# Two SwiGLU feed-forwards: parts two and three through Strassen's seven products

## The chip, the cores and the metric

The kernel runs on one core of a Trainium2 chip. The metric is the time of one execution on the device in microseconds (us), 1309.17 as the median of three runs. Beside the runs there is a profile of one execution. In it PE is the matrix engine, PEld its loading of stationary operands, DVE, ACT and POOL are the vector, scalar and GpSimd engines, and SP issues most DMAs.

## The reference

Two decoder layers work on 512 tokens of width 1024 in float32. Layer 0 mixes by a convolution module, layer 1 by differential attention. Each is followed by a feed-forward of width 2816 and a gated embedding:

```
def swiglu(x, w_gate, w_up, w_down):
    return (jax.nn.silu(x @ w_gate) * (x @ w_up)) @ w_down

    for i in range(DEPTH):
        h = h + (conformer_conv or diff_attention of rms_norm(h))
        u = rms_norm(h, ffn_norm_g[i])
        h = h + swiglu(u, ffn_w_gate[i], ffn_w_up[i], ffn_w_down[i])
        gate = jax.nn.sigmoid(rms_norm(h, ple_norm_g[i]) @ ple_w_gate[i])
        h = h + gate * (p[i] @ ple_w_proj[i])
```

The feed-forward (`ffn`) is the only part that changes, in both layers.

## The kernel before

All activations lie transposed: a tile is 128 features by 512 tokens, and `h` is eight such tiles. Each float32 operand of a large product is split in a high part (rounded to the type fp32r) and a low part (the rest), and a product is three matmuls: low weight with high activation, high with low, high with high (`mm3`, lines L155 to L157). Weights come as tiles of 128 x 1024 numbers (512 KB). `weight()` loads one through SP (L145) into one of two `wraw` buffers, ACT casts the high part into one of four `whi` buffers (L148), and DVE subtracts to get the low part into one of four `wlo` buffers (L150).

The feed-forward goes through its 2816 hidden features in three parts of 8, 8 and 6 hidden tiles. For each hidden tile a gate tile and an up tile of weights are loaded. Each is multiplied with the eight normalised inputs `norm.u` (in the `A` buffers, split in two): 8 x 3 matmuls over 512 tokens. DVE takes the sums out of PSUM and scales them by the row norm `rb` (L582, L584), ACT applies Silu, DVE multiplies (L585), and the hidden tile is split into a `B` buffer (L587, L588). After each part `linear` multiplies the hidden tiles with eight tiles of the down projection and adds to `h` (L592). In the last part each finished `h` tile also starts the next norm (`chunk`, L169, L170, squares, and POOL's sums, L189).

PSUM has eight banks: four `mm`, two `sc` and two `tp`, each 128 x 512. The order of the instructions on each engine is set by a planner at build time. Each engine then works through its own list strictly in that order and waits on semaphores; DMAs of SP and POOL are issued in the order of those engines' lists. Buffers are named by a tag (`C3`, `wk`, ...) with a number of copies; who takes a buffer waits until its last reader is done.

Of the kernel before, what the change touches and what calls it, by code (L numbers as in the profile page):

```python
# [12 lines left out]
F32 = mybir.dt.float32  # L13
F32R = mybir.dt.float32r
AF = mybir.ActivationFunctionType
ALU = mybir.AluOpType
# [4 lines left out]
P = 128  # L21
S = 512
D = 1024
NC = D // P
# [52 lines left out]
PACK = True  # L77
E1 = True
GLO = 1
QKV = (("q", 0, (0, 0, 0, 0)), ("v", 0, (0, 1, 1, 0)), ("q", 1, (1, 1, 2, 2)), ("q", 2, (0, 1, 2, 0)), ("v", 1, (1, 2, 2, 2)), ("q", 3, (0, 2, 0, 1)))  # L80


@with_exitstack
def trunk(ctx, tc, xT, pT, wts, diag, dww, vec, rel, onehot, lamv, out):
    nc = tc.nc
    V, A, G, T = nc.vector, nc.scalar, nc.gpsimd, nc.tensor
# [19 lines left out]
    big = lambda dt=F32, shape=(P, S): sb(list(shape), "big", 5, dt)  # L106
    f = lambda ap: ap.bitcast(F32)
# [6 lines left out]
    def col(name, i=0):  # L114
        a, _ = VEC[name]
        return vt[:, a + i : a + i + 1]
# [7 lines left out]
    t = wk()[:, 0:P]  # L124
# [4 lines left out]
    t = tp()  # L129
# [4 lines left out]
    wnext = [0]  # L134
    loaded = [None]

    def weight(n=1024, pieces=1, between=(), eng=V, after=None):
        i = wnext[0]
        wnext[0] += 1
        raw = sb([P, 1024], "wraw", 2)  # L140
        hi = sb([P, 1024], "whi", 4, F32R)
        lo = sb([P, 1024], "wlo", 4, F32R)
        for k in range(pieces):
            cut = slice(k * n // pieces, (k + 1) * n // pieces)
            loaded[0] = nc.sync.dma_start(raw[:, cut], wts[i, :, cut])  # L145
            if k < len(between):
                between[k]()
            A.copy(hi[:, cut], raw[:, cut])  # L148
            with tc.issue_after(after.ins) if after else nullcontext():
                eng.tensor_tensor(lo[:, cut], raw[:, cut], f(hi[:, cut]), ALU.subtract)  # L150
        return hi, lo

    def mm3(acc, a, b, first, last):
        (ah, al), (bh, bl) = a, b
        T.matmul(acc, al, bh, start=first, stop=False)  # L155
        T.matmul(acc, ah, bl, start=False, stop=False)  # L156
        return T.matmul(acc, ah, bh, start=False, stop=last)  # L157

    def wpart(w, k):
        return tuple(t[:, k * P : (k + 1) * P] for t in w)  # L160
# [5 lines left out]
    h = [sb([P, S], f"h{c}", 1) for c in range(NC)]  # L166
# [66 lines left out]
    norm = Norm("conv_g")  # L233
# [36 lines left out]
    y = []  # L270
# [160 lines left out]
    for c in range(NC):  # L431
        wa, wg = pairs[c]
        if c == 0:
            pg = half(wg)
            norm.diagonal()
            pa = half(wa)
            rb = norm.rows()
# [3 lines left out]
        if c > 0:  # L441
            pg = half(wg)
# [5 lines left out]
        tg, ta = big(), big()  # L448
# [114 lines left out]
    linear(NC, z, add_conv, 3, first=(None, last_add[0], scaled[1]))  # L563


    def ffn(norm, after):
        rb = None
        for at, (f0, n) in enumerate(PARTS):
            hid = []
            for i in range(n):  # L570
                wg, wu = weight(), weight()
                pg, pu = mm(), mm()
                for k in range(NC):
                    mm3(pg, wpart(wg, k), norm.u[k], k == 0, k == NC - 1)
                if rb is None:
                    norm.diagonal()
                for k in range(NC):
                    mm3(pu, wpart(wu, k), norm.u[k], k == 0, k == NC - 1)
                if rb is None:
                    rb = norm.rows()  # L580
                tg, tu = big(), big()
                V.tensor_tensor(tg, pg, rb, ALU.mult)  # L582
                A.activation(tg, tg, AF.Silu)
                V.tensor_tensor(tu, pu, rb, ALU.mult)  # L584
                V.tensor_tensor(tu, tu, tg, ALU.mult)  # L585
                hl = sb([P, 2, S], f"B{i}", 1, F32R)
                A.copy(hl[:, 0], tu)  # L587
                V.tensor_tensor(hl[:, 1], tu, f(hl[:, 0]), ALU.subtract)  # L588
                hid.append((hl[:, 0], hl[:, 1]))

            def add(m, acc):
                V.tensor_tensor(h[m], acc, h[m], ALU.add)  # L592
                if at == len(PARTS) - 1:
                    after.chunk(m)

            linear(n, hid, add, 2)

# [26 lines left out]
                gate(*part)  # L624

    n2 = Norm("ple_g0")
    ffn(norm, n2)
    norm = Norm("attn_g")
    ple(n2, pp, lambda m, cut: norm.chunk(m))

# [9 lines left out]
    for k in range(2):  # L640
        t = tp()
# [263 lines left out]
    norm = Norm("ffn_g1")  # L905
# [4 lines left out]

    linear(NC, ot, add_attn, 2, heads_until, step)
    n2 = Norm("ple_g1")
    ffn(norm, n2)

    def store(m, cut):
        nc.sync.dma_start(out[m][:, cut], h[m][:, cut])
# [30 lines left out]
def _layout(a):  # L947
# [25 lines left out]
    qkv = a["attn_w_qkv"][0]  # L973
    for what, at, _ in QKV:
        if what == "v":
# [70 lines left out]
```

## Time and profile before

| what | value |
|---|---|
| runs (median, lowest, highest) | 1309.17, 1309.03, 1310.07 us |
| the profiled execution, first to last instruction | 1308.0 us |
| what lies around that span, against the median | 1.2 us |
| PE busy | 1278.6 us (98%) in 5904 matmuls |
| DVE, ACT, POOL busy | 741.2 (57%), 522.1 (40%), 248.2 (19%) us |
| mean granted PE clock | 0.985 |
| DMA | 131.97 MB, 101 GB/s on average |

The feed-forward of layer 0 lies from about 230 to 584 us of the span (parts: hidden tiles to 316, 442 and 551, a down projection behind each), that of layer 1 from about 905 to 1258 us. A row of instruction groups names the line, engine and operation, what it writes and reads, its shape and count; then busy time, mean length of one in ns, and the idle time of the engine before it with what ended that. A busy PE is one with a matmul in its pipe; its pace is read from the starts of matmuls that follow each other.

### The profile page before, as it was taken

How to read it: one execution, taken by the hardware profiler on the slowest of the kernel's cores; microseconds unless marked ns; L12 is line 12 of the kernel's file. 1: busy time of each engine (PE TensorE's matmuls, PEld its weight loads, DVE VectorE, ACT ScalarE, POOL GpSimd, SP SyncE). 2: the span in 40 equal slices, each digit the busy share in tenths (PEclk: the TensorE clock that was granted, in tenths of full speed). 3: DMA queues.
4: the chain of work that ended last, by engine and by line, in shares of the span. 5: the costliest groups of instructions: out<-in, count | busy, mean ns of one | idle time of the engine just before them, and what ended most of it. 6: DMA issues, size and time to landing. Idle time of an engine off the chain costs nothing. (4 is left out here: it accounts for less than half of the span.)

```text
span 1308.0 us, 15405 instructions
## 1 busy us (share of the span) xinstructions
PE 1278.6 (98%) x5904; PEld 1055.7 (81%) x5904; DVE 741.2 (57%) x1142; ACT 522.1 (40%) x827; POOL 248.2 (19%) x207
## 2 busy tenths in 40 slices
PE   8999999999999999999999998999999999999998
PEld 5888678888888888888888886878888888888887
DVE  6898646444344434456678888845543344334445
ACT  5642445332122212254566667734332233223332
POOL 4754323000000000032335535122000000000030
PEclk8999889999999999999999998999999999999999
DMA  6654313322323232232222211213323223222231
GB/s 219 229 166 156 106 33 129 96 98 87 106 96 97 88 104 94 80 122 83 80 91 92 89 58 59 87 48 114 97 97 97 97 97 97 97 97 89 83 119 65
DMA packets 46838, 131.97 MB, mean 101 GB/s; under 512 B 5379, under 2 KB 9987, under 8 KB 46764
## 3 DMA queue, kind: packets, MB, share of 16 engines
q1 hardware_dynamic: 44640, 127.55, 29.6%
q10 hardware_dynamic: 2124, 3.43, 0.8%
q8 instruction: 46, 0.75, 0.2%
q14 instruction: 28, 0.23, 0.1%
HBM read 126.75 MB, written 4.21 MB: 100 GB/s over the span
## 5 line engine op out<-in xcount | busy, mean ns | idle before, releaser
L148 ACT CAST whi<-wraw 128x1024 fp32r<-128x1024 f32 (+2 forms) x214 | 218.6, 1026 | 566.3 <-PE mm L157 349.5
L155 PE MATMUL mm<-A,wlo 128*128 128x512 f32 (+1 forms) x1096 | 423.9, 391 | 4.8 <-ACT A L169 2.7
L156 PE MATMUL mm<-A,whi 128*128 128x512 f32 (+1 forms) x1096 | 428.0, 392 | 0.4
L157 PE MATMUL mm<-A,whi 128*128 128x512 f32 (+1 forms) x1096 | 425.3, 389 | 0.0
L150 DVE TENSOR_TENSOR wlo<-wraw,whi 128x1024 fp32r<-128x1024 f32 (+2 forms) x210 | 260.5, 1244 | 70.9 <-ACT whi L148 70.6
L155 PEld LDWEIGHTS mm<-A,wlo 128*128 128x128 f32 x1096 | 206.2, 188 | 49.6 <-DVE wlo L150 3.7
L156 PEld LDWEIGHTS mm<-A,whi 128*128 128x128 f32 x1096 | 206.6, 188 | 46.4 <-DVE A L170 3.0
L157 PEld LDWEIGHTS mm<-A,whi 128*128 128x128 f32 x1096 | 206.6, 188 | 43.1 <-issue 1.0
L189 POOL TENSOR_TENSOR acc<-acc,wk 128x512 f32<-128x512 f32 x42 | 67.4, 1604 | 787.7 <-issue 660.2
L156 PE MATMUL mm<-B,whi 128*128 128x512 f32 x352 | 137.5, 391 | 0.0
L157 PE MATMUL mm<-B,whi 128*128 128x512 f32 x352 | 137.5, 391 | 0.0
L155 PE MATMUL mm<-B,wlo 128*128 128x512 f32 x352 | 137.2, 392 | 0.0
L592 DVE TENSOR_TENSOR h<-mm,h 128x512 f32<-128x512 f32 x48 | 33.0, 691 | 122.7 <-PE mm L157 122.7
L584 DVE TENSOR_TENSOR big<-mm,rb 128x512 f32<-128x512 f32 x44 | 30.4, 691 | 126.2 <-PE mm L157 126.2
L582 DVE TENSOR_TENSOR big<-mm,rb 128x512 f32<-128x512 f32 x44 | 30.4, 691 | 99.4 <-PE mm L157 93.0
L157 PEld LDWEIGHTS mm<-B,whi 128*128 128x128 f32 x352 | 66.1, 188 | 14.6
L155 PEld LDWEIGHTS mm<-B,wlo 128*128 128x128 f32 x352 | 66.1, 188 | 14.2
L156 PEld LDWEIGHTS mm<-B,whi 128*128 128x128 f32 x352 | 66.0, 188 | 14.2
L157 PE MATMUL mm<-whi,A 128*128 128x512 f32 x192 | 75.6, 395 | 0.0
L156 PE MATMUL mm<-wlo,A 128*128 128x512 f32 x192 | 75.0, 396 | 0.0
L155 PE MATMUL mm<-whi,A 128*128 128x512 f32 x192 | 74.8, 397 | 0.0
L214 POOL TENSOR_TENSOR r<-v,mhalf 128x8 f32<-128x8 f32 (+1 forms) x31 | 47.4, 1529 | 122.8 <-DVE v L212 100.4
(198 smaller groups left out, 1402.0 us busy)
## 6 DMA issues: line engine op xcount, KB each, us to landing
wraw<-in_wts SPq DMA_DIRECT2D x194, 512.0 KB, 3.5
wraw<-in_wts SPq DMA_DIRECT2D x16, 384.0 KB, 2.9
D<-in_diag SPq DMA_DIRECT2D x22, 256.0 KB, 4.9
C<-in_diag SPq DMA_DIRECT2D x16, 256.0 KB, 4.7
h<-in_xT SPq DMA_DIRECT2D x8, 256.0 KB, 5.6
bias<-scr ACTq DMA_DIRECT2D x8, 256.0 KB, 3.3
out_t<-h SPq DMA_DIRECT2D x7, 256.0 KB, 2.0
wraw<-in_wts SPq DMA_DIRECT2D x4, 256.0 KB, 5.2
```

Of the source, the lines that this page charges most:

```text
L148: A.copy(hi[:, cut], raw[:, cut])
L150: eng.tensor_tensor(lo[:, cut], raw[:, cut], f(hi[:, cut]), ALU.subtract)
L155: T.matmul(acc, al, bh, start=first, stop=False)
L156: T.matmul(acc, ah, bl, start=False, stop=False)
L157: return T.matmul(acc, ah, bh, start=False, stop=last)
L189: self.last = self.eng.tensor_tensor(self.acc, self.acc, sq, ALU.add)
L214: last_pow[0] = G.tensor_tensor(r[:, :n], v[:, :n], mhalf[:, :n], ALU.pow)
L582: V.tensor_tensor(tg, pg, rb, ALU.mult)
L584: V.tensor_tensor(tu, pu, rb, ALU.mult)
L592: V.tensor_tensor(h[m], acc, h[m], ALU.add)
```

## The change

Part one of each feed-forward stays as it was. In parts two and three hidden tiles are made in pairs. The gate weights of a pair are a matrix of 256 columns by 1024 rows, and the input is 1024 by 512 tokens. Each is taken as 2 x 2 blocks (two hidden tiles; the upper and lower 512 inputs; the first and last 256 tokens), and their product is formed by Strassen's scheme: seven products of block sums in place of eight, with sums of the results. Each of the seven products is 4 x 3 matmuls over 256 tokens. The same holds for the up weights. So a pair has two calls of `strassen`, a feed-forward has 14 calls (8 in part two, 6 in part three), and the kernel 28.

- **Input sums.** `combinations()` makes the seven input operands from the scaled input (`h * gain * rb`, so the results need no scaling by `rb`) once per feed-forward, in steps that `feed()` releases under part one. Operands 1, 6 and 7 take the `A` buffers and are made when part one's products have read them; the others lie in `C`, `D` and `wth`/`wtl` buffers.
- **Weight sums.** `operands()` loads two tiles, `r1` and `r2`, through SP (L644, L646). POOL issues a DMA that adds half of `r2`'s tile in memory onto the other half of `r2` (256 KB, L647), computes two block sums into `d` (L649, L650), and issues a DMA that adds the second tile onto `r1` (512 KB, L653) after `r1`'s own block has been split for product 3. The splits (L636 on ACT, L637 on DVE) are one half tile for product 3 and three full tiles: for products 2 and 4, for 1 and 5, for 6 and 7.
- **Result sums.** `strassen()` runs the products in the order 3, 4, 2, 5, 1, 6, 7 and adds the results on ACT (L677, L682, L683) and DVE (L680, L684, L685, L688).
- `r1` has three buffers in turn: two `wraw`, and a `C4` at every third call.

```diff
+H2 = S // 2
+PLAIN = ((0,0),(0,1),(0,2),(0,3))
+PACE = 2
+        def combinations():
+            ...
+            for name, x, y, op in (
+                (3, b22, b12, ALU.subtract), (4, b11, b21, ALU.subtract), (2, b11, None, None), (5, b22, None, None),
+                (1, b11, b22, ALU.add), (6, b11, b12, ALU.add), (7, b21, b22, ALU.add),
+            ):
+                if name in LATE:
+                    while (0, len(done_pairs) - 1) in PLAIN and (0, len(done_pairs)) in PLAIN:
+                        yield
+                ...
+                for j in range(2):
+                    t = x[j]
+                    if y:
+                        t = wk(F32, (P, 2, H2))
+                        G.tensor_tensor(t, x[j], y[j], op)
+                    A.copy(his[j], t)
+                    V.tensor_tensor(los[j], t, f(his[j]), ALU.subtract)
+                    ...
+                    yield
+        def two_parts(raw):
+            ...
+            A.copy(hi, raw)
+            V.tensor_tensor(lo, raw, f(hi), ALU.subtract)
+            ...
+        def operands(i):
+            turn[0] += 1
+            r1 = sb([P, 1024], "C4" if turn[0] % 3 == 0 else "wraw", 2)
+            nc.sync.dma_start(r1, wts[i])
+            r2 = sb([P, 1024], rtags, 2)
+            nc.sync.dma_start(r2, wts[i + 2])
+            nc.gpsimd.dma_start(r2[:, :S], wts[i + 2, :, S:], accum_op=ALU.add)
+            d = sb([P, 1024], dtags[turn[0] % 2], 2)
+            G.tensor_tensor(d[:, :S], r1[:, :S], r2[:, S:], ALU.subtract)
+            G.tensor_tensor(d[:, S:], r1[:, :S], r1[:, S:], ALU.add)
+            w = {}
+            (w[3],) = two_parts(r1[:, :S])
+            nc.gpsimd.dma_start(r1, wts[i + 2], accum_op=ALU.add)
+            w[2], w[4] = two_parts(r2)
+            w[1], w[5] = two_parts(d)
+            w[6], w[7] = two_parts(r1)
+            return w
+        def strassen(i, b):
+            w = operands(i)
+            def product(acc, name):
+                for k in range(4):
+                    mm3(acc, wpart(w[name], k), b[name][k], k == 0, k == 3)
+            vp, qp, mp, xp = mm(), mm(), tp(), sc()
+            product(vp[:, H2:], 3)
+            product(vp[:, :H2], 4)
+            o1, o2 = big(), wk()
+            A.copy(o2, vp)
+            product(qp[:, H2:], 2)
+            product(qp[:, :H2], 5)
+            V.tensor_tensor(halves(o2), swapped(qp), halves(o2), ALU.subtract)
+            product(mp[:, :H2], 1)
+            A.copy(o1[:, :H2], mp[:, :H2])
+            A.mul(o1[:, H2:], mp[:, :H2], -1.0)
+            V.tensor_tensor(o1, vp, o1, ALU.add)
+            V.tensor_tensor(o1, o1, qp, ALU.subtract)
+            product(xp[:, H2:], 6)
+            product(xp[:, :H2], 7)
+            V.tensor_tensor(o1, xp, o1, ALU.add)
+            return o1, o2
         for at, (f0, n) in enumerate(PARTS):
+            for pair in range(n // 2):
+                if (at, pair) in PLAIN:
+                    ... (as before, with feed(PACE) behind a hidden tile)
+                gs = strassen(i, comb)
+                for t in gs:
+                    A.activation(t, t, AF.Silu)
+                us = strassen(i + 1, comb)
+                for o, (t, g) in enumerate(zip(us, gs)):
+                    V.tensor_tensor(t, t, g, ALU.mult)
+                    ... (split into the pair's B buffers: A.copy, V.tensor_tensor)
```

The planner's lists change as follows; outside the feed-forwards they stand as before. A row names the line, the operation, what it writes and reads, and the size; the numbers of the lines are those of the kernel that is shown.

PE in part two, before: the last third of an up tile's 24 matmuls.

```order
L155 MATMUL mm_558_3124<-A8_323_1650,wlo_556_3119 128x512
L156 MATMUL mm_558_3124<-A9_324_1651,whi_555_3118 128x512
L157 MATMUL mm_558_3124<-A8_323_1650,whi_555_3118 128x512
L155 MATMUL mm_558_3124<-A10_330_1689,wlo_556_3119 128x512
L156 MATMUL mm_558_3124<-A11_331_1690,whi_555_3118 128x512
L157 MATMUL mm_558_3124<-A10_330_1689,whi_555_3118 128x512
```

PE in part two, now: the end of product 5 of the fourth call and the beginning of its product 1 (`wth`, `wtl` and `A` hold the input sums, L164 to L166 are `mm3`).

```order
L164 MATMUL mm_577_3102<-wth_435_2255,wlo_573_3094 128x256
L165 MATMUL mm_577_3102<-wtl_437_2257,whi_572_3093 128x256
L166 MATMUL mm_577_3102<-wth_435_2255,whi_572_3093 128x256
L164 MATMUL tp_578_3103<-A0_460_2404,wlo_573_3094 128x256
L165 MATMUL tp_578_3103<-A2_462_2406,whi_572_3093 128x256
L166 MATMUL tp_578_3103<-A0_460_2404,whi_572_3093 128x256
```

Matmuls of 512 tokens became matmuls of 256, in the ratio 168 for 96 per pair.

DVE in part two, before: one hidden tile is five rows and two splits.

```order
L582 TENSOR_TENSOR big_493_2747<-mm_491_2697,rb_360_1848 128x512
L150 TENSOR_TENSOR wlo_509_2829<-wraw_507_2827,whi_508_2828 128x1024
L584 TENSOR_TENSOR big_494_2748<-mm_492_2698,rb_360_1848 128x512
L585 TENSOR_TENSOR big_494_2748<-big_494_2748,big_493_2747 128x512
L150 TENSOR_TENSOR wlo_512_2835<-wraw_510_2833,whi_511_2834 128x1024
L588 TENSOR_TENSOR B1_495_2753<-big_494_2748,B1_495_2753 128x512
```

DVE in part two, now: the fourth call (an up call). The first row is the split for products 1 and 5 of that call, the third the one for its products 6 and 7, the fourth and fifth the first splits of the fifth call.

```order
L637 TENSOR_TENSOR wlo_573_3094<-C3_567_3081,whi_572_3093 128x1024
L688 TENSOR_TENSOR big_563_3005<-sc_562_2980,big_563_3005 128x512
L637 TENSOR_TENSOR wlo_575_3098<-wraw_565_3076,whi_574_3097 128x1024
L637 TENSOR_TENSOR wlo_588_3215<-wraw_584_3206,whi_587_3214 128x512
L637 TENSOR_TENSOR wlo_590_3220<-C5_585_3208,whi_589_3219 128x1024
L680 TENSOR_TENSOR wk_581_3130<-mm_577_3102,wk_581_3130 128x512
L730 TENSOR_TENSOR wk_581_3130<-wk_581_3130,wk_564_3006 128x512
L684 TENSOR_TENSOR big_580_3129<-mm_576_3101,big_580_3129 128x512
L637 TENSOR_TENSOR wlo_592_3224<-C3_586_3211,whi_591_3223 128x1024
L685 TENSOR_TENSOR big_580_3129<-big_580_3129,mm_577_3102 128x512
L734 TENSOR_TENSOR B3_547_2951<-wk_581_3130,B2_546_2950 128x2x256
L688 TENSOR_TENSOR big_580_3129<-sc_579_3104,big_580_3129 128x512
```

The split for products 6 and 7 of a call (it reads `r1` after the adding DMA) stands directly ahead of the split for product 3 of the next call.

POOL, before: between the norm ahead of the feed-forward (the end of its sums and `r8`) and the last part's norm it has nothing.

```order
L189 TENSOR_TENSOR acc_291_1463<-acc_291_1463,wk_332_1693 128x512
L189 TENSOR_TENSOR acc_291_1463<-acc_291_1463,wk_339_1732 128x512
L189 TENSOR_TENSOR acc_291_1463<-acc_291_1463,wk_346_1771 128x512
L214 TENSOR_TENSOR r8_358_1820<-v8_357_1818,mhalf_4_71 128x4
L189 TENSOR_TENSOR acc_347_1774<-acc_347_1774,wk_672_3925 128x512
L189 TENSOR_TENSOR acc_347_1774<-acc_347_1774,wk_679_3958 128x512
```

POOL, now, in the middle of part two, for the third and fourth call: the adding DMA onto `r2`, the two block sums, the adding DMA onto the `r1` of the call before.

```order
L647 DMA C5_549_2954<-in_wts 128x512
L649 TENSOR_TENSOR C3_550_2957<-C4_548_2952,C5_549_2954 128x512
L650 TENSOR_TENSOR C3_550_2957<-C4_548_2952 128x512
L653 DMA wraw_529_2822<-in_wts 128x1024
L647 DMA C5_566_3078<-in_wts 128x512
L649 TENSOR_TENSOR C3_567_3081<-wraw_565_3076,C5_566_3078 128x512
L650 TENSOR_TENSOR C3_567_3081<-wraw_565_3076 128x512
L653 DMA C4_548_2952<-in_wts 128x1024
```

The adding DMA onto a call's `r1` stands behind the block sums of the call after it.

More of the change, by code (lines that the diff above doesn't have):

```diff
@@ L79 @@
 GLO = 1
+H2 = S // 2
+LATE = {1: [(f"A{i}", 1, 2) for i in (0, 1, 2, 3)], 6: [(f"A{i}", 1, 2) for i in (4, 5, 6, 7)], 7: [(f"A{i}", 1, 2) for i in (8, 9, 10, 11)]}
+WT = [("wth", 2, 2), ("wth", 2, 2), ("wtl", 2, 2), ("wtl", 2, 2)]
+SPACE = (
+    ({3: [("C0", 2, 4)] * 2, 4: [("C1", 2, 4)] * 2, 2: [("C2", 2, 4)] * 2, 5: WT, **LATE}, "C5", ("C3", "C3"), ("C3", "C3", "C5", "C5")),
+    ({3: [("C0", 2, 4)] * 2, 4: [("C1", 2, 4)] * 2, 2: [(f"D{i}", 1, 2) for i in (0, 1, 4, 5)], 5: WT, **LATE}, "C5", ("C2", "C3"), ("C2", "C3", "C5", "C5")),
+)
+PLAIN = ((0,0),(0,1),(0,2),(0,3))
+PACE = 2
 QKV = (("q", 0, (0, 0, 0, 0)), ("v", 0, (0, 1, 1, 0)), ("q", 1, (1, 1, 2, 2)), ("q", 2, (0, 1, 2, 0)), ("v", 1, (1, 2, 2, 2)), ("q", 3, (0, 2, 0, 1)))
@@ L563, in trunk, with ffn, home, feed @@
     linear(NC, z, add_conv, 3, first=(None, last_add[0], scaled[1]))
-    def ffn(norm, after):
+    def ffn(norm, after, space):
+        homes, rtags, dtags, utags = space
         rb = None
+        def home(t, n, size):
+            if size == 4:
+                w = sb([P, 4, H2], t, n, F32R)
+                return [w[:, 0:2], w[:, 2:4]]
+            return [sb([P, 2, H2], t, n, F32R)]
+        comb = {}
+        def combinations():
+            us = []
+            for c in range(NC):
+                if c % 2 == 0:
+                    us.append(sb([P, 2, S], utags[c // 2], 2))
+                V.scalar_tensor_tensor(us[c // 2][:, c % 2], h[c], col(norm.g, c), rb, ALU.mult, ALU.mult)
+                if c % 4 == 3:
+                    yield
+            part = lambda k, t: [us[2 * k + j][:, :, t * H2 : (t + 1) * H2] for j in range(2)]
+            b11, b12, b21, b22 = part(0, 0), part(0, 1), part(1, 0), part(1, 1)
+            for name, x, y, op in (
[5 more added lines that the diff above has]
+                        yield
+                places = [home(*t) for t in homes[name]]
+                his, los = places[: len(places) // 2], places[len(places) // 2 :]
+                his, los = [t for p in his for t in p], [t for p in los for t in p]
+                for j in range(2):
[5 more added lines that the diff above has]
+                    V.tensor_tensor(los[j], t, f(his[j]), ALU.subtract)
+                    comb[name] = [(his[k // 2][:, k % 2], los[k // 2][:, k % 2]) for k in range(2 * len(his))]
+                    yield
+        def feed(n=1):
+            for _ in range(n):
+                if making:
+                    try:
+                        next(making[0])
+                    except StopIteration:
+                        making.pop()
+        done_pairs = []
+        making = [combinations()]
+        turn = [0]
+        def two_parts(raw):
+            n = raw.shape[-1]
+            hi = sb([P, 1024], "whi", 4, F32R)[:, :n]
+            lo = sb([P, 1024], "wlo", 4, F32R)[:, :n]
+            A.copy(hi, raw)
+            V.tensor_tensor(lo, raw, f(hi), ALU.subtract)
+            return [tuple(t[:, j : j + S] for t in (hi, lo)) for j in range(0, n, S)]
+        def operands(i):
[15 more added lines that the diff above has]
+            return w
+        def swapped(t):
+            return bass.AP(t.tensor, t.offset + H2, [list(t.ap[0]), [-H2, 2], [1, H2]])
+        def halves(t):
+            return t.rearrange("p (a s) -> p a s", a=2)
+        def strassen(i, b):
[20 more added lines that the diff above has]
+            return o1, o2
@@ L568, in ffn @@
         for at, (f0, n) in enumerate(PARTS):
             hid = []
[L570 to L589, printed above, removed]
+            for pair in range(n // 2):
+                hi, lo = (sb([P, 2, S], f"B{2 * pair + k}", 1, F32R) for k in range(2))
+                for k in range(2):
+                    hid.append((hi[:, k], lo[:, k]))
+                if (at, pair) in PLAIN:
+                    for i in range(2):
+                        wg, wu = weight(), weight()
+                        pg, pu = mm(), mm()
+                        for k in range(NC):
+                            mm3(pg, wpart(wg, k), norm.u[k], k == 0, k == NC - 1)
+                        if rb is None:
+                            norm.diagonal()
+                        for k in range(NC):
+                            mm3(pu, wpart(wu, k), norm.u[k], k == 0, k == NC - 1)
+                        if rb is None:
+                            rb = norm.rows()
+                        tg, tu = big(), big()
+                        V.tensor_tensor(tg, pg, rb, ALU.mult)
+                        A.activation(tg, tg, AF.Silu)
+                        V.tensor_tensor(tu, pu, rb, ALU.mult)
+                        V.tensor_tensor(tu, tu, tg, ALU.mult)
+                        A.copy(hi[:, i], tu)
+                        V.tensor_tensor(lo[:, i], tu, f(hi[:, i]), ALU.subtract)
+                        if i == 1:
+                            done_pairs.append(pair)
+                        if pair > 0 or i == 1:
+                            feed(PACE)
+                    continue
+                while making and any(at == 0 and (at, p) in PLAIN for p in range(pair)):
+                    feed()
+                i = wnext[0]
+                wnext[0] += 4
+                gs = strassen(i, comb)
[4 more added lines that the diff above has]
+                    V.tensor_tensor(t, t, g, ALU.mult)
+                    step = H2 - S if o else H2 + S
+                    hs, ls = (bass.AP(x.tensor, x.offset + (S if o else 0), [list(x.ap[0]), [step, 2], [1, H2]]) for x in (hi, lo))
+                    A.copy(hs, halves(t))
+                    V.tensor_tensor(ls, halves(t), f(hs), ALU.subtract)
@@ L594, in add @@
                     after.chunk(m)
+                feed()
             linear(n, hid, add, 2)
```

4 lines of the change are left out of this document (2 added, 2 removed).

## The prediction

> **What bounds the kernel.** I read the page's busy shares first, then the stretches of a feed-forward, the waits in part two, and the starts of single matmuls. Busy share (us, share of the span, instructions):
>
> ```profile
> PE 1278.6 (98%) x5904; PEld 1055.7 (81%) x5904; DVE 741.2 (57%) x1142; ACT 522.1 (40%) x827; POOL 248.2 (19%) x207
> ```
>
> Stretches of layer 0's feed-forward: length, busy time per engine (instructions), granted PE clock, DMA share, GB/s. The first is most of part one, the second a down projection, the third part two:
>
> ```profile
> 240.00:316.00 76.00, 76.00 (x336) 62.90 (x336) 37.59 (x46) 23.90 (x30) 0.00 (x0) 1.00 0.29 97
> 316.00:357.00 41.00, 41.00 (x180) 33.55 (x179) 15.14 (x16) 8.32 (x8) 0.00 (x0) 1.00 0.27 90
> 357.00:442.00 85.00, 85.00 (x377) 70.39 (x376) 37.57 (x45) 24.48 (x31) 0.00 (x0) 1.00 0.30 99
> ```
>
> PE never pauses there, at full granted clock. Who waits is DVE (waiter, waited for, us, times, longest):
>
> ```profile
> DVE big L584 <- PE mm L157: 24.7, 8, 3.1
> DVE big L582 <- PE mm L157: 18.7, 8, 3.2
> ```
>
> So time in a feed-forward is the number of matmuls times their pace, and the others have room: DVE 44% busy (37.57 of 85), POOL idle. The pace for 512 tokens, and for 256 where the kernel's last tile is cut in two (start, length, engine):
>
> ```profile
> 1297.01 0.39 PE L155 MATMUL mm<-A,wlo 128*128 128x512 f32 x1
> 1297.24 0.39 PE L156 MATMUL mm<-A,whi 128*128 128x512 f32 x1
> 1297.46 0.39 PE L157 MATMUL mm<-A,whi 128*128 128x512 f32 x1
> 1297.69 0.28 PE L155 MATMUL mm<-A,wlo 128*128 128x256 f32 x1
> ...
> 1303.20 0.28 PE L156 MATMUL mm<-A,whi 128*128 128x256 f32 x1
> ```
>
> The first four start 0.227 us apart. From 1297.69 to 1303.20 there are 46 steps: 0.1198 us each. A hidden tile confirms the long one (48 matmuls, 10.88 us, 0.2267 each):
>
> ```profile
> 381.77 0.69 DVE L582 TENSOR_TENSOR big<-mm,rb 128x512 f32<-128x512 f32 x1 [2.21 <-PE mm L157]
> 392.65 0.69 DVE L582 TENSOR_TENSOR big<-mm,rb 128x512 f32<-128x512 f32 x1 [2.22 <-PE mm L157]
> ```
>
> **PE.** A pair was 96 x 0.2267 = 21.76 us and becomes 168 x 0.1198 = 20.13. Half the tokens cost 53% of the time, so of Strassen's eighth about three fifths are left: 1.63 us a pair, 0.82 a call. 14 pairs: **22.8 us**, all on the path, since PE ends it everywhere here. A call takes 10.07 us, a product 1.44.
>
> **Input sums.** Per feed-forward eight scalings on DVE, ten sums on POOL, 14 splits on ACT and DVE: about 8 x 0.75 + 14 x 0.69 = 16 us of DVE, spread over part one and its down projection (some 120 us, DVE about half busy). I cost them at nothing: DVE's and ACT's waits for PE hide them. The last three are made while the last plain tile frees the `A` buffers; product 1 first reads them a down projection (8 x 24 matmuls, 43.5 us) later. Uncovered they would cost up to 16 us a layer, but no row brings them near.
>
> **DVE in a call.** The prices (line, engine, output and inputs, count, busy time, mean ns):
>
> ```profile
> L150 DVE TENSOR_TENSOR wlo<-wraw,whi 128x1024 fp32r<-128x1024 f32 x15 | 18.3, 1222 | 3.5 <-ACT whi L148 3.5
> L592 DVE TENSOR_TENSOR h<-mm,h 128x512 f32<-128x512 f32 x48 | 33.0, 691 | 122.7 <-PE mm L157 122.7
> L588 DVE TENSOR_TENSOR B<-big,B 128x512 fp32r<-128x512 f32 x44 | 30.1, 685 | 1.4 <-ACT B L587 1.4
> L148 ACT CAST whi<-wraw 128x1024 fp32r<-128x1024 f32 x16 | 16.9, 1053 | 58.9 <-issue 31.2 <-PE mm L157 27.8
> L583 ACT ACTIVATE big<-big 128x512 f32<-128x512 f32 x8 | 5.0, 626 | 0.0
> ```
>
> Splits 3 x 1.22 + 0.69, four result sums of 0.69, and half a pair's multiplications and splits (2 x 0.69): 8.5 us in 10.07. ACT: casts 3 x 1.05, and six shorter ones (half a tile's cast, copies, Silu or `B` casts) at no more than 0.63: 6.9 us. Both fit, DVE with 1.6 us to spare. Does its order fit? Let a call begin at T. The split for the next call's products 2 and 4 needs a `whi` buffer that product 2 frees at T + 4.3, a cast, and itself: done at T + 6.6. From there to the split for products 6 and 7 itself included, the list has six rows of 0.69 and two of 1.22: T + 13.2, or 3.1 us into the next call; with waits for ACT's copies I put it at 3.8. Product 6 begins at 7.2. So 3.4 us are free, and the other splits have more.
>
> **POOL beside DVE.** Two block sums a call, and DVE's splits read two operands from SBUF as they do. What that does is on record where POOL adds squares (start, length):
>
> ```profile
> 224.85 1.21 DVE L150 TENSOR_TENSOR wlo<-wraw,whi 128x1024 fp32r<-128x1024 f32 x1
> 225.98 1.77 DVE L170 SCALAR_TENSOR_TENSOR A<-h,vec,A 128x512 fp32r<-128x512 f32 x1
> 225.03 2.18 POOL L189 TENSOR_TENSOR acc<-acc,wk 128x512 f32<-128x512 f32 x1 [4.62 <-ACT wk L188]
> 208.15 1.29 POOL L189 TENSOR_TENSOR acc<-acc,wk 128x512 f32<-128x512 f32 x1 [4.30 <-ACT wk L188]
> 222.87 0.74 DVE L560 SCALAR_TENSOR_TENSOR h<-mm,vec,h 128x512 f32<-128x512 f32 x1
> ```
>
> POOL took 2.18 in place of 1.29, DVE 1.77 where the same operation with one input in PSUM took 0.74: they went one after the other. Two sums a call can hold DVE up by 0 to 2 x 1.29 = 2.6 us, against 1.6 to spare. The four result sums read PSUM and can run beside POOL, and DVE must wait for casts anyway, so I take half, 1.3, and no stall. The Trainium skill ("SBUF — State Buffer", "SBUF: two separate sides") has the pair of ports as an exclusive lock held for a whole instruction; the rows agree.
>
> **The adding DMAs.** None is in the trace. Nearest rows (from SP, KB each, us from issue to landing):
>
> ```profile
> wraw<-in_wts SPq DMA_DIRECT2D x194, 512.0 KB, 3.5
> wraw<-in_wts SPq DMA_DIRECT2D x16, 384.0 KB, 2.9
> ```
>
> Below, an addition of 512 KB costs a plain load, 3.5. Above, it reads and writes back one after the other, 7.0, and POOL needs another 2.2 (its longest sum above) to send it: 9.2. I take twice the bytes by the slope (512 KB more is 4 x 0.6 = 2.4): 5.9, and 0.6 for POOL: **6.5 us**, nearest the idea that target and source are read side by side. The Trainium skill ("Collectives: The Full Stack", "The bandwidth ceiling: the fold count and why AG ≠ RS ≠ AR") says that an addition in a DMA costs two source reads and no more. With the fixed 2.0 us and bytes/436e3 of "DMA: Bandwidth & Descriptors" ("Anatomy of one DMA — SWDGE (gpsimd) path") that makes an estimate of 4.4, and the sum stays the same.
>
> Who waits: the addition onto a call's `r1` stands on POOL behind the next call's block sums. These wait for a `d` buffer (free at about T) and for `r2` (freed at T - 3.5, loaded in 3.5), and take 2.6. The addition also waits for `r1`'s split for product 3 on DVE, which ends at 3.8 + 0.69. So it goes out at T + 4.5 and lands at T + 11, 0.9 us into the call that uses it. Cast and split end by 3.8, as above. Behind that split on DVE stands the one for product 3 of the next call, which releases the next addition: a loop of DMA + 1.05 + 1.22 + 0.69. With 6.5 it takes 9.5 us, under 10.07; it becomes the pace when the DMA takes over **7.1 us**.
>
> The small addition onto `r2` (256 KB) goes out at about T and its split comes over 10 us later: nothing. Memory traffic rises: two loads and 0.75 of two loads' bytes added, 1.84 MB in 10.07 us, 182 GB/s. The page's row by slices shows more in its second one:
>
> ```profile
> GB/s 219 229 166 156 106 33 129 96 98 87 106 96 97 88 104 94 80 122 83 80 91 92 89 58 59 87 48 114 97 97 97 97 97 97 97 97 89 83 119 65
> ```
>
> So I cost the traffic at nothing beyond what it may do to the length of an addition.
>
> **Seams.** Four runs of calls (8, 6, 8, 6) begin and end at a down projection. Its tiles take 5.44 us with four buffers ahead, and the first call's `r1`, `d` and addition fit into its last three; at the end four hidden tiles or more of the down projection cover the last pair's sums. I allow 1 us in all, from 0 to 1 per seam.
>
> **Sum.** 1308.0 + 1.2 around the span = 1309.2, the median; - 22.8 + 1 = **1287.4 us**.
>
> **Rivals.**
> - *DVE is full.* If every block sum holds DVE for its whole 1.29, a call asks 8.5 + 2.6 = 11.1 us, 1.0 over. Each run has 3.4 us to lose first: 28 x 1.0 - 4 x 3.4 = 14.4 lost, 1301.8; with 0.7 over, 6 lost, 1293. For it: the row of 1.77. Against: POOL may start only behind the split that frees `d`, next to rows that read PSUM.
> - *The addition is late, a little.* A loop that is s over per call loses 28 s - 13.6 on PE. If sending it waits for a DVE split of 1.22, as POOL's sums do, 6.5 becomes 7.7, s 0.6: 3 lost, 1291; with 8.0 it is 11.6, 1299. The rows of POOL's sums speak for it, none for a DMA. [...]
> - *Slower.* The same loop decides from s = 1.3 (28 x 1.3 - 13.6 = 22.8), a DMA of 8.4 us. At 9.2 the loop takes 12.2 us, s = 2.1, 45 us lost: **1333**. For it: the trace has packets but no POOL-issued DMA, and the loads of `r1` and `r2` run at the same time; longest wait for a weight load:
>
> ```profile
> 816.43 4.67 DMA wraw<-in_wts
> ```
>
> That is 1.2 over the median even for plain ones. Against: 8.4 is 2.4 times the plain load.
> - *No gain in the matmuls.* If 256 tokens cost what weights' loading costs (188 ns by the mean of PEld), calls would be slower; excluded by the 0.1198 above, with the same kind of operands:
>
> ```profile
> L155 PEld LDWEIGHTS mm<-A,wlo 128*128 128x128 f32 x1096 | 206.2, 188 | 49.6 <-DVE wlo L150 3.7
> ```
>
> **How the numbers follow.** This kernel's runs lie within 0.1%, so 0.2% (2.6 us) is about what a measurement tells from no change. Full pace 0.53; DVE full 0.15; the addition a little late 0.11; within 0.2% of 1309.2, as losses happen to match, 0.05; slower 0.16. The forecast is the first case's, 1287.4, its own range 1284 to 1291 (1286.4 with nothing lost at seams, less 2 for spread and rounding of the pace; above, half of the eight seams at 1 us each). The range for 8 in 10 takes in the second and third case: 1284 to 1308. Faster 0.79, same 0.05, slower 0.16.
>
> **What the changed profile would show.** If right: in parts two and three matmuls of 256 start 0.12 us apart without idle time on PE, calls 10.1 us apart, DVE 85 to 95% busy, additions of 512 KB landing 6 to 7 us after issue, POOL's sums stretched to about 2 us now and then. If DVE is the limit: PE waits for the low part of a split, and DVE has no idle time. If the addition is: the same wait, but DVE and ACT stand before it waiting for a DMA, and calls are DMA + 3 us apart. Wrong altogether if PE's clock falls or input sums hold up part one.

## The result, and the profile after

The changed kernel takes 1348.66 us (median of 4 runs, 1336.54 to 1352.59), the kernel before 1309.36 beside it (1309.03 to 1310.07): 1.029 times as long, 95% interval 1.024 to 1.034. It is slower by 39 us where 22 us less were forecast. The profiled execution took 1347.41 us.

The page's busy times of the changed kernel, in the same columns as before:

```profile
PE 1271.9 (95%) x6912; PEld 1099.1 (82%) x6912; DVE 923.0 (69%) x1298; ACT 608.4 (45%) x995; POOL 406.5 (30%) x339
```

PE has 1008 matmuls more (shorter ones) and is busy 7 us less, but the span grew by 38: PE now waits. The stretches of layer 0's feed-forward show where (length; PE, PEld, DVE, ACT, POOL busy; clock; DMA share; GB/s):

```profile
240.00:316.00 76.00, 76.00 (x337) 62.96 (x336) 58.12 (x66) 30.45 (x42) 19.29 (x12) 1.00 0.36 110
316.00:357.00 41.00, 41.00 (x197) 34.24 (x196) 16.06 (x17) 9.09 (x10) 11.28 (x10) 1.00 0.43 102
357.00:442.00 85.00, 73.61 (x575) 72.91 (x575) 65.25 (x66) 37.31 (x59) 27.82 (x25) 0.94 0.64 147
```

Part one and its down projection are as full as before, although the input sums are made there (DVE 58.12 us in place of 37.59, POOL 19.29 in place of none). In part two PE is busy 73.61 of 85 us, and DVE, with 65.25, isn't full either. Who waits (waiter, waited for, us, times, longest):

```profile
PE sc L164 <- DVE wlo L637: 40.6, 13, 4.6
```

`sc` is the bank of products 6 and 7, so PE waits for their split. The chain of waits in the middle of layer 1's part two (start, length, what) shows why that split is late:

```profile
1074.66 7.62 DMA wraw<-in_wts
...
1082.37 1.05 ACT whi L636
...
1085.33 1.23 POOL C L650
1086.56 2.28 issue
1088.84 8.08 DMA wraw<-in_wts
...
1097.02 1.06 ACT whi L636
...
1099.90 1.22 POOL C L650
1101.12 2.28 issue
1103.40 7.89 DMA C<-in_wts
```

It repeats: the additions go out 13.9 to 14.7 us apart, and PE isn't in it. An addition onto `r1` lands, ACT casts, POOL's second block sum ends, and 2.28 us later the next addition goes out. What stands in that "issue" is on the timelines of DVE, POOL and SP (start, length, engine, line):

```profile
1088.17 1.21 DVE L637 TENSOR_TENSOR wlo<-C,whi 128x1024 fp32r<-128x1024 f32 x1
1098.10 4.10 DVE L637 TENSOR_TENSOR wlo<-wraw,whi 128x1024 fp32r<-128x1024 f32 x1 [3.86 <-ACT whi L636]
1102.13 0.68 DVE L637 TENSOR_TENSOR wlo<-C,whi 128x512 fp32r<-128x512 f32 x1
1088.84 0.90 POOL L653 DMA_DIRECT2D wraw<-in_wts  x1 [2.29 <-issue]
1097.73 0.86 POOL L647 DMA_DIRECT2D C<-in_wts  x1 [7.99 <-DMA C<-in_wts]
1098.29 1.61 POOL L649 TENSOR_TENSOR C<-wraw,C 128x512 f32<-128x512 f32 x1
1099.54 1.57 POOL L650 TENSOR_TENSOR C<-wraw 128x512 f32<-128x512 f32 x1
1087.72 0.33 SPq L644 DMA_DIRECT2D wraw<-in_wts  x1
1089.45 0.33 SPq L646 DMA_DIRECT2D C<-in_wts  x1
```

- The split for products 6 and 7 has its operands at 1098.10 but takes 4.10 us in place of 1.22. It ends 1.1 us after POOL's second sum (1101.11): both sums went ahead of it. The split for the next product 3 then follows (0.68), and 0.6 later, at 1103.40, the next addition.
- POOL's sums come just then because they waited 7.99 us for the load of `r2`. SP sent that load at 1089.45, when the split at 1088.17 (for products 2 and 4) had ended and freed its buffer: 0.6 us after the addition onto `r1`. A load of a later `r1` had gone out at 1087.72, as soon as the split for 6 and 7 had ended. So one stretch of DVE's list releases three transfers within 1.7 us; addition and `r2` take about 8 us each and land within 0.8 us of each other, at 1096.92 and 1097.73.

Two loops thus share DVE's row: split for 6 and 7, split for product 3, addition, cast; and split for 2 and 4, load of `r2`, sums, which hold the split for 6 and 7. The addition's loop adds up to 8.08 + 0.1 + 1.05 + 4.10 + 0.68 + 0.6 = 14.6 us, where a call of PE needs 10.07. In other calls the sums fall one row later. Ten of the 28 splits for 6 and 7 took 3.7 to 4.3 us in this trace, and in five other calls it was the split for product 3 behind it that took 3.5 to 3.8 in place of 0.68. Both rows are in the loop.

### The profile page after: what moved, and what is told of

Same layout as the page of the kernel before. It is cut to its first block, busy times and chain, and to the rows that moved or that the text cites. A ratio compares the mean times of both kernels' runs of the same rounds, so it can differ in the third digit from the quotient of the medians.

```text
span 1345.6 us, 18205 instructions
## 1 busy us (share of the span) xinstructions
PE 1271.9 (95%) x6912; PEld 1099.1 (82%) x6912; DVE 923.0 (69%) x1298; ACT 608.4 (45%) x995; POOL 406.5 (30%) x339
## 5 line engine op out<-in xcount | busy, mean ns | idle before, releaser
L164 PE MATMUL mm<-A,wlo 128*128 128x512 f32 (+1 forms) x648 | 249.6, 392 | 5.3 <-ACT A L178 2.7
L165 PE MATMUL mm<-A,whi 128*128 128x512 f32 (+1 forms) x648 | 253.4, 393 | 0.3
L166 PE MATMUL mm<-A,whi 128*128 128x512 f32 (+1 forms) x648 | 251.2, 389 | 0.0
L159 DVE TENSOR_TENSOR wlo<-wraw,whi 128x1024 fp32r<-128x1024 f32 (+2 forms) x154 | 195.8, 1276 | 59.5 <-ACT whi L157 59.1
L164 PEld LDWEIGHTS mm<-A,wlo 128*128 128x128 f32 x648 | 122.4, 189 | 32.4 <-DVE wlo L159 4.2
L165 PEld LDWEIGHTS mm<-A,whi 128*128 128x128 f32 x648 | 122.5, 189 | 29.1 <-DVE A L179 3.4
L166 PEld LDWEIGHTS mm<-A,whi 128*128 128x128 f32 x648 | 122.4, 189 | 25.5 <-issue 1.0
L164 PE MATMUL mm<-B,wlo 128*128 128x512 f32 x352 | 136.3, 392 | 3.3 <-DVE wlo L159 3.3
L166 PE MATMUL mm<-B,whi 128*128 128x512 f32 x352 | 137.1, 390 | 0.0
L637 DVE TENSOR_TENSOR wlo<-C,whi 128x1024 fp32r<-128x1024 f32 (+1 forms) x72 | 105.5, 1468 | 34.6 <-ACT whi L636 34.6
L636 ACT CAST whi<-C 128x1024 fp32r<-128x1024 f32 (+1 forms) x72 | 72.0, 1001 | 93.2 <-PE mm L166 62.3
L164 PE MATMUL sc<-A,wlo 128*128 128x256 f32 x224 | 71.3, 318 | 40.6 <-DVE wlo L637 40.6
L637 DVE TENSOR_TENSOR wlo<-wraw,whi 128x512 fp32r<-128x512 f32 (+1 forms) x40 | 63.4, 1605 | 45.6 <-ACT whi L636 45.6
L164 PE MATMUL mm<-C,wlo 128*128 128x256 f32 (+1 forms) x296 | 86.2, 291 | 0.0
L165 PE MATMUL mm<-C,whi 128*128 128x256 f32 (+1 forms) x296 | 85.8, 290 | 0.0
L166 PE MATMUL mm<-C,whi 128*128 128x256 f32 (+1 forms) x296 | 85.7, 290 | 0.0
L164 PEld LDWEIGHTS sc<-A,wlo 128*128 128x128 f32 x224 | 49.7, 222 | 42.9 <-issue 42.9
```

The lines of the kernel that those rows point to most:

```text
L636: A.copy(hi, raw)
L637: V.tensor_tensor(lo, raw, f(hi), ALU.subtract)
```

## The experiments

Times are medians; the ratio is to the kernel before, run beside, with its 95% interval. The kernel before took 1307.5 to 1310.1 us in these sessions, so differences between times of two sessions are good to some 3 us.

**1. Without the addition onto `r1`** (products 6 and 7 then use `r1` alone; POOL's block sums stay).

```diff
-            nc.gpsimd.dma_start(r1, wts[i + 2], accum_op=ALU.add)
```

> Leaves out the 512 KB addition onto r1 (products 6 and 7 then get r1's plain blocks); all else stays, POOL's block sums too. In the changed kernel's trace a call takes up to 14.5 us and runs in a loop: addition sent, landed 7 to 8.6 us later, cast 1.05, split held to 4.1 by two block sums of POOL, next split 0.68, next addition. If the long addition is the cause: no loop is left, calls take 10.1 us, 1285 to 1295 us. If POOL's block sums beside DVE are the cause: DVE still asks about 11 us a call, 1300 to 1320 us. If the PE clock (0.213 us steps behind a pause) is a cause of its own: the slow steps stay, over 1310.

1286.54 us, 0.984 (0.983 to 0.986). That is the forecast's pace, with both block sums in. So the addition is necessary for the loss, and the sums alone cost next to nothing. They hold splits here too, even longer on average than in the changed kernel (2419 ns against 1973, shown below at experiment 11). In a stretch of layer 1's part two (columns as above) DVE is busy 62.75 of 67 us, and PE still doesn't pause:

```profile
L637 DVE TENSOR_TENSOR wlo<-wraw,whi 128x1024 fp32r<-128x1024 f32 x20 | 48.4, 2419 | 1.5 <-ACT whi L636 0.8
```
```profile
1031.00:1098.00 67.00, 67.00 (x552) 66.44 (x550) 62.75 (x66) 36.86 (x58) 18.71 (x16) 1.00 0.49 134
```

So a held split cost time in this kernel only where a loop waits for it.

**2. The same DMA as a plain copy** (`r1` is overwritten in place of added to; every engine's list is unchanged).

```diff
-            nc.gpsimd.dma_start(r1, wts[i + 2], accum_op=ALU.add)
+            nc.gpsimd.dma_start(r1, wts[i + 2])
```

> The same DMA from POOL with the same bytes and the same order of everything, but a plain copy, without the addition (products 6 and 7 get the second tile alone). If the addition itself makes the DMA long: it lands about 5 us after issue instead of 7.2, the loop falls under or near 10.1 us, 1287 to 1300. If it is the sending by POOL or the meeting with the load of r2: still about 7 us and 1330 to 1350. If the block sums hold the loop: 1320 to 1340.

1293.58 us (1289.20 to 1307.50), 0.991 (0.988 to 0.994). From issue to landing (KB, us), the copy here and the addition in the changed kernel:

```profile
wraw<-in_wts POOLq DMA_DIRECT2D x20, 512.0 KB, 4.2
```
```profile
wraw<-in_wts POOLq DMA_DIRECT2D x20, 512.0 KB, 7.2
```

With the waits, the order and the sums as they were, 3 us less of transfer took away 55 of the 62 us that lie between 1348.66 and experiment 1.

**3. Block sums only once** (both additions stay; POOL computes `d` for the first call of a feed-forward, the later calls use that one).

```diff
-            d = sb([P, 1024], dtags[turn[0] % 2], 2)
-            G.tensor_tensor(...)   # both
+            if not once:
+                d = ...; G.tensor_tensor(...)   # both
+                once.append(d)
+            d = once[0]
```

> Both additions stay; POOL's two block sums are made only at the first call of a feed-forward and used by all its calls (products 1 and 5 are then of the wrong weights), with all splits as before. If the long addition alone is the cause: loop 8.0 + 1.05 + 1.22 + 0.68 + 0.6 = 11.6 us, 1.5 over, 28 x 1.5 - 13.6 = 28 us over full pace: 1310 to 1320. If the sums that stand before the split are needed for the loss: 1287 to 1300.

1302.15 us, 0.996 (0.994 to 0.997). The chain in layer 1's part two now shows the addition's loop alone:

```profile
1062.55 7.89 DMA wraw<-in_wts
...
1070.54 1.06 ACT whi L637
...
1072.76 0.70 DVE wlo L638
1073.46 0.35 issue
1073.80 9.02 DMA C<-in_wts
```

From one addition to the next it is 11.25 us; the split is back at its 1.22. So 46 of the 62 us need the sums that hold the split, and 16 are left to a long addition by itself.

**4. Neither** (experiments 1 and 3 together: no addition onto `r1`, and the sums left out after the first call).

> Leaves out both the addition onto r1 and, behind the first call of a feed-forward, the block sums. All theories of the weights' path expect full pace here, 1309.2 - 22.8 + 0 to 4: 1286 to 1290. If it is over 1295, something else costs (PE's clock, input sums, seams).

1286.95 us, 0.985 (0.983 to 0.987), as in experiment 1. The sums cost only together with the addition.

**5. The split for the next product 3 ahead of the one for products 6 and 7.** `operands` becomes a generator in three steps (up to the addition; splits for 2, 4, 1, 5; split for 6, 7), and the next call's first step is written ahead of this call's third. Nothing is left out.

```diff
+            next(g)               # splits for products 2, 4 and 1, 5
+            if later:
+                begin(later)      # loads, sums, split for 3, addition of the next call
+            next(g)               # split for products 6, 7
```

> Everything is computed as in the changed kernel; only the order differs: the next call's cast and split for product 3 stand on ACT and DVE ahead of this call's cast and split for products 6 and 7. POOL's order is as before. Theory (a loop closed by DVE's order: addition, cast, split for 6 and 7, split for the next product 3, next addition): the loop is cut, since the addition of the next call no longer waits for the addition of this one; calls 10.1 to 10.5 us apart and 1287 to 1297 us, with splits still held by POOL's sums now and then. Rival 1 (POOL's own queue: the addition stands behind the next call's block sums and is late whatever DVE does): calls stay above 12.5 us, 1325 us or more. Rival 2 (DVE is full once the loop is gone, 8.5 us and 2.6 of POOL's sums per call): calls 11.1 us, about 1302.

1297.39 us (1293.86 to 1299.90), 0.991 (0.988 to 0.993). One split moved ahead on DVE, past a result sum and the split for 6 and 7, and its cast on ACT, are worth 51 of the 62 us. POOL's order was unchanged, so its queue was not what cost these 51.

**6. Both orders**: as 5, and on POOL the addition onto `r1` goes out ahead of the next call's small addition and sums.

```diff
+            with tc.issue_after(added[0].ins) if added else nullcontext():
                 nc.gpsimd.dma_start(r2[:, :S], wts[i + 2, :, S:], accum_op=ALU.add)
                 G.tensor_tensor(...)   # both
```

> Everything is computed; the split for the next product 3 is ahead as in the last kernel, and on POOL the addition onto a call's r1 is sent ahead of the next call's small addition and block sums. Theory (loop by DVE's order): no faster than the last kernel by more than 4 us, 1287 to 1297, since the loop is already cut. Rival 1 (POOL's queue): this one is clearly faster than the last, which would stand at 1325 or more. If the sums, now behind the sending, come late for the split for products 1 and 5, it is slower than the last by 5 us or more.

1294.19 us, 0.989 (0.987 to 0.991); against experiment 5 the intervals overlap. What is left can be read in the stretches shown at experiment 9.

**7. POOL's order alone.**

> Everything is computed; DVE and ACT keep the changed kernel's order, and only on POOL the addition onto a call's r1 is sent ahead of the next call's small addition and block sums, so that these sums run while the addition is under way and no longer meet the split for products 6 and 7. Theory (loop by DVE's order, 46 us of its loss from the sums that hold the split): the loop stays with 7.4 to 8.5 for the addition and 3.0 for the two splits and the cast, and 0.2 to 0.5 of waits: calls 10.7 to 12.3 us, 1296 to 1312. Rival (sums hold the split wherever they stand, since POOL's two are always late): calls stay at 13 to 15, 1330 to 1349.

1307.84 us, 0.999 (0.997 to 1.001). The sums now run while the addition is under way, and the split for 6 and 7 takes 1.22 again; the loop by DVE's order stays, with additions of 7.1 us in the median. Calls in the middle of a run take 11.4 to 12.6 us, a smaller loss per call, as in experiment 3. So 41 of the 62 us go with every sum still made, only because the sums stand elsewhere on POOL.

**8. Both orders, and one of POOL's two block sums as a load and an adding DMA** (256 KB each). Nothing is left out.

```diff
+            nc.sync.dma_start(d[:, S:], wts[i, :, :S])
-                G.tensor_tensor(d[:, S:], r1[:, :S], r1[:, S:], ALU.add)
+                nc.gpsimd.dma_start(d[:, S:], wts[i, :, S:], accum_op=ALU.add)
```

> Everything is computed, with the two orders of the last experiments (split for the next product 3 first on DVE, addition onto r1 first on POOL). In addition one of the two block sums of a call is no longer POOL's: SP loads its first summand into d (256 KB) and an adding DMA puts the second on it (256 KB). DVE was 94% busy in the kernel with both orders, calls 11.0 to 11.2 us apart. Theory (what is left, 1294 against 1287 without addition, is DVE held by POOL's sums): one sum less frees 1.3 us of DVE per call, 28 x 0.7 or so back, splits of 128x1024 at about 1.4 us on average in place of 1.6, and 1286 to 1291 us. Rival (what is left is the traffic, 166 to 173 GB/s at a DMA share of 0.7): 0.5 MB more per call makes the additions longer and late, PE waits again for the split for 6 and 7, and the time is 1297 or more.

1286.63 us (1284.34 to 1287.42), 0.983 (0.981 to 0.984).

**9. Both orders, block sums only once** (the later ones left out).

> Both orders as in the last experiments and both additions, but POOL computes its two block sums only for the first call of a feed-forward; all calls use those. So the later sums are left out. Theory (what is left is DVE held by POOL's sums): full pace, calls 10.1 us apart, 1285 to 1289 us, with the additions at 5.5 to 7.5 us. Rival (traffic or the additions): 1292 to 1296 as with the sums.

1286.69 us, 0.983 (0.981 to 0.985). The same stretch of layer 1's part two in experiments 6, 8 and 9 (columns as above):

```profile
1031.00:1098.00 67.00, 65.23 (x534) 64.12 (x533) 63.29 (x61) 36.07 (x56) 26.06 (x24) 1.00 0.69 166
```
```profile
1031.00:1098.00 67.00, 67.00 (x554) 66.70 (x553) 59.01 (x65) 38.63 (x59) 22.62 (x23) 1.00 0.91 226
```
```profile
1031.00:1098.00 67.00, 67.00 (x560) 67.00 (x559) 52.35 (x65) 39.14 (x60) 10.47 (x12) 1.00 0.74 182
```

In 6 DVE is busy 63.29 of 67 us and PE pauses; with one sum less on POOL, or both, DVE has room and PE doesn't pause. So the last 7.5 us of experiment 6 need POOL's sums. They need the addition as well, since experiment 1, with both sums and DVE as busy (62.75 of 67), has PE at 67.00. What makes the two together cost these 7.5 us was not tried. Experiment 8 keeps PE full at a DMA share of 0.91 and 226 GB/s: traffic alone is not a limit. It is the fastest version that leaves nothing out.

**10. One sum as a DMA, in the changed kernel's order.**

> Everything is computed, in the changed kernel's order on DVE and ACT; as in the fastest experiment, one of a call's two block sums is made by a load and an adding DMA of 256 KB each instead of by POOL. Theory (loop by DVE's order, with the held split as one term): the split for 6 and 7 is held by one POOL sum instead of two, about 2.6 us in place of 4.1, but POOL now sends one DMA more (0.9) ahead of the addition and there is more traffic beside it; calls 13 to 14 us, 1315 to 1340, far from the 1287 of the same edit with the loop cut. Rival (the sum as DMA was all that mattered, the orders little): 1287 to 1300.

1342.89 us, 1.027 (1.021 to 1.034), a little more than expected. The additions and PE's wait:

```profile
wraw<-in_wts POOLq DMA_DIRECT2D x20, 512.0 KB, 7.6
```
```profile
PE sc L164 <- DVE wlo L637: 36.4, 14, 5.7
```

The edit that is worth 7.5 us with the loop cut is worth about 6 with the loop closed, less than the spread of these runs. The hold of the split became shorter (1735 ns on average in place of 1973), the additions longer (7.6 us in place of 7.2).

**11. `r2` loaded only for the first two calls of a feed-forward** (24 of 28 loads left out; the small addition goes onto what the buffers hold; the order of all other rows is the changed kernel's).

> The changed kernel's order, row for row; r2 is loaded by SP only for the first two calls of a feed-forward, the small addition then goes onto what these buffers hold, so that 24 of 28 loads of r2 are left out. Theory 1 (the addition onto r1 is long because the load of r2 runs beside it: 8.1 us in the loop, 5.2 to 5.8 where it runs alone): additions of 512 KB at 5.2 to 6.2 us, the loop 2 us or more shorter, 1295 to 1325. Theory 2 (7 to 8 us is what an addition takes in the loop, whatever runs beside it): median still 7 us or more, and 1330 to 1349.

1288.66 us, 0.984 (0.982 to 0.986), faster than either theory said. Additions, and the split of `wraw` tiles for 6 and 7 (mean ns of one behind the busy time), here and in the changed kernel:

```profile
wraw<-in_wts POOLq DMA_DIRECT2D x20, 512.0 KB, 6.4
```
```profile
L637 DVE TENSOR_TENSOR wlo<-wraw,whi 128x1024 fp32r<-128x1024 f32 x20 | 26.5, 1326 | 22.4 <-ACT whi L636 22.3
```
```profile
L637 DVE TENSOR_TENSOR wlo<-wraw,whi 128x1024 fp32r<-128x1024 f32 x20 | 39.5, 1973 | 45.6 <-ACT whi L636 45.6
```

Taking that one load away does both things: additions shrink from 7.2 to 6.4, and the split from 1973 ns to 1326, since POOL's sums no longer wait for a load that lands with the addition: POOL waited for loads of `r2` 22 times, 155.1 us in all, in the changed kernel, and 3 times, 5.6 us, here. So the load of `r2`, the second loop, is as necessary for the loss as the addition. Which of its two effects weighs more this run doesn't part. The second was not in the expectation, which counted only the shorter addition.

## Why the prediction was wrong

Right were the parts that set the forecast's size.

- *PE.* Where nothing holds PE, the kernel takes 1286.5 to 1286.7 us (experiments 1, 8, 9), 1287.4 forecast. That is 21.3 to 21.7 us less than the kernel before beside them, where 21.8 were forecast; pace and seams were not measured apart.
- *Input sums* at nothing: the stretch of part one is full, 76.00 of 76.00, and in layer 1's part one PE doesn't pause either.
- *Traffic* at nothing for PE: experiment 8 at 226 GB/s.
- *DVE in a call*: 8.5 us in 10.07 and no stall by itself. In experiment 9 it was busy 52.35 of 67 us, 7.9 in 10.07. The first rival had POOL's two sums fill DVE, at 1293 to 1301.8. Experiment 6 lies there, at 1294.19, but that is no proof of it: in experiment 1 the same sums left PE at full pace.

Wrong were two steps of the path for the addition onto `r1`.

- *POOL beside DVE: "I take half, 1.3, and no stall."* The sums were costed as a share of DVE's time, not as a delay at a place in the loop. They fell on rows for which a loop waits. In the chain above that is the split for 6 and 7, held for 2.9 us (4.10 against 1.22). The Trainium skill ("SBUF — State Buffer", "SBUF: two separate sides") has the loser of the shared ports block until the winner's whole instruction is over; the row of 4.10 agrees, and shows more, since the second sum too went ahead of the waiting split. By experiment 3 this is worth 46 of the 62 us, by experiment 7 41.
- *The adding DMAs: "target and source are read side by side", 6.5 us.* The median was 7.2 us, and 7.6 onto the `C4` buffers. The length goes with the loads sent around it: the six of 28 in the changed kernel with no load sent from 5 us before to 4 us after them took 5.2 to 5.8, the others up to 8.8; in experiment 6, where most have a load sent 1.1 us or more behind them and none right ahead, the median is 5.6. The traffic was costed at nothing "beyond what it may do to the length of an addition", and that was then not costed. The wait for `r2` was put at "freed at T - 3.5, loaded in 3.5"; in the trace the same stretch of DVE's list releases addition and loads, so they meet in call after call. An estimate of 4.4 stood in the prediction from the Trainium skill's pages; no run shows an addition as short (the shortest took 5.1), and the plain copy alone took 4.2.

The loop that failed was the prediction's own, DMA + 1.05 + 1.22 + 0.69, with 7.1 us for the DMA as the point where it becomes the pace; the rival *Slower* put 8.4 us for the point from which it decides. By the measured 7.2 the sum would have given 0.1 us over, within the 3.4 us that each run may lose, so 1287 still. Only with the held split in it (2.9), 0.6 from the last split's end to the sending, and an addition of 8.08 does it come to the 14.6 of the trace. That would be 28 x 4.5 - 13.6 = 112 us by the prediction's formula. 62 were lost, 12.8 a call by the same formula, since only the middle calls of a run stand in the full loop: the first addition of layer 1's part two took 5.8 us, and in part three product 6 began every 10.1 to 14.9 us. So the rival with 16 in 100 had the right mechanism, a loop that decides. Its term was wrong: it needed an addition of 8.4 or more, the median was 7.2, and the held split made up the difference. The time, 1349, lay outside its 1333 and outside the range.

The rival *The addition is late, a little* had the sending wait for a DVE split. In the rows above it doesn't: the sending at 1088.84 took 0.90 us beside the split of 1088.17 to 1089.38.

## What to carry to other kernels

Where a row on one engine releases a transfer that a later row of the same engine waits for, add up the whole loop, with every other engine that can hold a row in it, and compare it with the pace; an average share of "1.3 us in 10" says nothing there. Look what else the same moment releases: here transfers sent within 1.7 us of each other took longer and landed together. The cheap remedy is the order: the split that releases the next transfer, written ahead of the row that waits for the last one, was worth 51 us here.

## What was not expected of the hardware

**A pause of PE can be followed by matmuls at half the pace.** Matmuls on PE around the wait in the loop above (start, length):

```profile
1099.29 0.28 PE L166 MATMUL tp<-A,whi 128*128 128x256 f32 x1
1102.35 0.55 PE L164 MATMUL sc<-A,wlo 128*128 128x256 f32 x1 [2.78 <-DVE wlo L637]
1102.70 0.41 PE L165 MATMUL sc<-A,whi 128*128 128x256 f32 x1
1102.91 0.41 PE L166 MATMUL sc<-A,whi 128*128 128x256 f32 x1
...
1105.44 0.28 PE L166 MATMUL sc<-A,whi 128*128 128x256 f32 x1
1105.56 0.28 PE L164 MATMUL sc<-A,wlo 128*128 128x256 f32 x1
```

After 2.78 us without work, matmuls of 256 start 0.213 us apart until 1105.26 and then 0.12 again. The 14 steps from 1102.35 to 1105.44 take 3.09 us, 1.4 more than at 0.12, and the granted clock of this stretch is 0.51. The Trainium skill ("TensorE: Matmul & The Clock Gate", Part 1) has half the clock after an idle window of about 3.4 us; here 2.78 was enough. The length of the pause alone doesn't decide: after one of 3.05 us, which ended at 383.44, the matmuls start 0.12 apart from the second on, at a granted clock of 1.00. After one of 2.32, which ended at 1073.61, the clock was 0.50 from 1074.66 to 1078.07. As PE stands outside the loop, this is not shown to have cost time of its own.

**An addition sent 1 us ahead of a load kept its length.** From the issues and landings of single DMAs: a 512 KB addition with no load sent from 5 us before to 4 us after it took 5.2 to 6.1 us in 34 of 38 cases (7.5 to 7.7 in the other four; all runs with additions), with a load sent 1.0 to 2.2 us behind it 5.1 to 6.6 in 38 of 39 cases (7.0 in the other; experiments 6 and 9), with one sent 0.4 to 0.7 us behind it 7.2 to 7.7 (experiments 6 and 8, eight cases), and with one 1.1 us ahead and one 1.2 behind 7.6 to 8.8 (changed kernel, seven cases). The load behind pays too: loads of `r1` sent behind an addition took 4.8 to 7.7 in experiment 6, 3.5 in the row of plain loads before. What does it was not tried.
